# Queries of five heads as seven block products, the softmax ratio on GpSimd, and a step of attention in a lone unit's gap

## The chip, the cores and the metric

The kernel runs on one core of a Trainium2 chip. Its time is the device time of one execution in microseconds (us). Five engines matter: TensorE (PE in the profile, PEld for its weight loads), VectorE (DVE), ScalarE (ACT), GpSimd (POOL) and SyncE (SP), which issues most DMAs. Each engine runs its own list of instructions strictly in the order of that list and waits, where an operand isn't there yet, with all that stands behind it.

## The reference

A trunk of two layers on 16 learned meta tokens and 512 tokens of width 1024: first gated linear attention, then differential attention. The change is in the second layer, cut here to its core:

```python
proj = xn @ w_in                                  # (528, 1024) @ (1024, 8192)
q, k, v, z = jnp.split(proj, 4, axis=-1)          # 8 heads, two maps of 128 each
lam = exp(sum(lv[0]*lv[1])) - exp(sum(lv[2]*lv[3])) + lambda_init
# for each block of 128 queries:
s = einsum('bhpqd,bhpkd->bhpqk', qb, kh) * scale + bias   # p: map 0 and map 1
p = softmax(where(dist >= 0, s, -inf))
a = p[:, :, 0] - lam * p[:, :, 1]
o = einsum('bhqk,bhkv->bhqv', a, vh)
o = head_rms(o) * gnorm * (1.0 - lambda_init)
y = silu(z) * o
h = h + y @ w_out
```

## The kernel before

Every fp32 operand of a matmul is split into a high and a low part (ScalarE copies the high part, VectorE subtracts it for the low part, `split`, L276 and L277), and a product is high by high, high by low and low by high.

The eight heads run one after another. TensorE's order is written out by the program: a queue (`Weaver`) holds the projections of the next head as generators, and the loop over heads places the steps of this head's attention between pieces of them. `W.fill(us)` runs pieces from the queue until their written costs have used up `us`. The order of the other engines is made when the program is built, from priorities and assumed durations; it is a fixed list by the time it runs.

A projection of 256 columns is done in one of two ways. Plain (`project`, L421): for each of two halves of 128 columns 24 matmuls, over all tokens at once (512 columns for queries). Or as a `Unit` of seven block products (`product`, L431): tokens and weights are each cut in two by two blocks, VectorE makes sums of weight blocks (L366), and seven products p1 to p7 of 12 matmuls each, over half of the tokens (256 columns, or 264 with meta tokens), stand for eight. ScalarE copies running sums out of a bank as `u` (L452: after p1, p6 and p7, which add up in one bank bx), and VectorE forms the four outputs from a bank and `u` (L477, L479). The weights come as the parts a11, a12, a22 (used in p1, p2, p4), s21 (p5, p6) and s43 (p7, p3). Only two buffers exist for the last kind, so s43 is made when an earlier pair has been used up. p3 adds up in p5's bank bv, once VectorE has read it for p7's output.

A unit whose successor in the queue is a unit too runs that one's p1 inside itself. A unit that was begun so (`early`) and has no unit behind it is called lone here: its order is p6, p5, p7, p2, p4, p3.

In the second layer gates (z), values (v) and keys (k) are units, in that order, and queries (q) are plain in all heads; from head 2 on each head begins with the output projection of an earlier pair of heads (`q_diff_out2`, its matmuls at L400), and in head 6 the order is k, q, v, z.

Attention of a block of 128 queries has four steps: A (`scores`: for both maps the scores on TensorE at L400, evicted with the bias and the running minimum by VectorE at L1692, the exponential with its sum on ScalarE at L1694; then the ratio of the sums at L1697 and L1698 and the combined tile at L1699), B (`turn`, transposes, L1707), C (`values`, with a power on GpSimd for the norm, L1730), E (`rows`, L1737 and L1740). They are placed as A3 A2 B3 A1 C3 B2 E3 A0 C2 B1 E2 C1 B0 E1 C0 E0, by blocks counted from 0.

The gate unit's p5, as it is written before:

```python
            def p5():
                self.bv = pb_tile("bv")
                yield from product(self.bv, ws.use(s21)[1], X["t1"])
```

## Time and profile before

| what | value |
|---|---|
| time, median of 3 runs (lowest to highest) | 971.22 us (970.94 to 971.46) |
| the profiled execution's own time | 970.65 us |
| its span in the trace | 968.9 us |
| TensorE busy | 957.2 us (99%) |
| VectorE busy | 778.6 us (80%) |
| ScalarE busy | 626.8 us (65%) |
| GpSimd busy | 44.9 us (5%) |
| granted TensorE clock | 0.999 |

The span is the time from the first to the last instruction; what is missing to the execution's time lies around it. Busy times are unions of the instructions' durations on an engine. Matmuls overlap in the array, so for TensorE the distance from start to start tells the cost, not the duration of one.

### The profile page before, as it was taken

Reading aid. Unit: us, or ns where it says so; the run is one execution under the profiler, and the core shown is the slowest. Engines: PE = TensorE matmul, PEld = TensorE weight load, DVE = VectorE, ACT = ScalarE, POOL = GpSimd, SP = SyncE. Lnnn points to the kernel's source line nnn. Section 1 sums busy time; section 2 is a strip of 40 time slices with the busy share of each in tenths; the row PEclk is TensorE's granted clock in tenths of the full one; section 3 lists DMA queues with packets and bytes.
Section 4 is the critical chain, followed back from the end, with each engine's and each line's share of the span. In section 5 each row is a group of like instructions: output and inputs, shape, how many; then the busy total and the mean of one; then the engine's idle time right before and its main releaser. Section 6 shows DMA issues by size and latency. Waiting matters only on the chain.

```text
span 968.9 us, 18048 instructions
## 1 busy us (share of the span) xinstructions
PE 957.2 (99%) x6993; PEld 906.9 (94%) x6993; DVE 778.6 (80%) x1586; ACT 626.8 (65%) x1304; POOL 44.9 (5%) x68
## 2 busy tenths in 40 slices
PE   9999999999999999999999999999999999999997
PEld 8999999999999999998899998998999989989996
DVE  7989885886888787668997987968869769687785
ACT  7776755577647567656757776575675756755583
POOL 1000000000000000000001001000000000000001
PEclk9999999999999999999999999999999999999999
DMA  7322223635363236124355525243342341722212
GB/s 197 88 85 59 82 79 122 147 103 128 116 162 91 85 117 158 53 101 152 99 130 138 143 73 133 75 139 98 99 138 88 118 119 44 182 70 84 89 64 87
DMA packets 128522, 104.94 MB, mean 108 GB/s; under 512 B 51102, under 2 KB 112830, under 8 KB 128433
## 3 DMA queue, kind: packets, MB, share of 16 engines
q1 hardware_dynamic: 123104, 93.80, 35.1%
q10 hardware_dynamic: 5328, 9.95, 2.8%
q8 instruction: 56, 0.92, 0.4%
q14 instruction: 34, 0.27, 0.1%
HBM read 83.64 MB, written 11.80 MB: 99 GB/s over the span
## 4 chain that ended last, share of the span: by engine, by line
PE 88%; ACT 1%; DVE 1%; issue 1%; POOLq 0%; DVEq 0%
PE bx L431 19%; PE bv L431 12%; PE by L431 10%; PE bx L421 10%; PE ps L400 9%; PE bx L972 5%; PE bx L400 3%; PE bv L972 2%; PE by L972 2%; PE ps L1214 2%; PE by L400 2%; PE bv L400 2%; PE ps L1807 1%; PE bx L1807 1%; PE bv L421 1%; PE by L421 1%
## 5 line engine op out<-in xcount | busy, mean ns | idle before, releaser
L277 DVE TENSOR_TENSOR wl<-raw,wh 128x1024 fp32r<-128x1024 f32 x98 | 119.4, 1221 | 23.0 <-ACT wh L276 18.9
L276 ACT ACTIVATE wh<-raw 128x1024 fp32r<-128x1024 f32 x98 | 103.1, 1054 | 48.3 <-PE by L972 22.9
L431 PE MATMUL bv<-x,wh 128*128 128x264 f32 (+1 forms) x656 | 98.6, 287 | 0.0
L431 PE MATMUL bx<-x,wh 128*128 128x264 f32 (+1 forms) x640 | 95.6, 286 | 0.0
L431 PEld LDWEIGHTS bv<-x,wh 128*128 128x128 f32 x656 | 86.8, 189 | 0.6 <-DVE z L479 0.2
L431 PEld LDWEIGHTS bx<-x,wh 128*128 128x128 f32 x640 | 84.6, 188 | 0.7 <-ACT u L452 0.2
L452 ACT ACTIVATE u<-bx 128x264 f32<-128x264 f32 (+1 forms) x120 | 45.3, 379 | 35.5 <-PE bx L431 33.1
L1694 ACT ACTIVATE p<-p,st 128x528 f32<-128x528 f32 (+3 forms) x64 | 36.5, 570 | 41.7 <-DVE st L1692 41.4
L421 PE MATMUL bx<-x,wh 128*128 128x512 f32 (+1 forms) x256 | 62.4, 385 | 0.0
L277 DVE TENSOR_TENSOR wl<-sum,wh 128x1024 fp32r<-128x1024 f32 x41 | 50.1, 1221 | 10.6 <-ACT wh L276 10.5
L431 PE MATMUL bx<-x,wl 128*128 128x264 f32 (+1 forms) x320 | 54.1, 284 | 0.0
L431 PE MATMUL bv<-x,wl 128*128 128x264 f32 (+1 forms) x328 | 53.8, 284 | 0.1
L421 PEld LDWEIGHTS bx<-x,wh 128*128 128x128 f32 x256 | 44.4, 188 | 7.8
L276 ACT ACTIVATE wh<-sum 128x1024 fp32r<-128x1024 f32 x41 | 43.1, 1051 | 9.7 <-PE by L972 3.9
L431 PE MATMUL by<-x,a12h 128*128 128x264 f32 (+1 forms) x320 | 47.5, 286 | 0.1
L1730 POOL TENSOR_TENSOR st<-st,mhalf 128x1 f32<-128x1 f32 x32 | 25.5, 795 | 468.6 <-ACT on L1728 418.2
L431 PE MATMUL bx<-x,a11h 128*128 128x264 f32 (+1 forms) x320 | 46.6, 284 | 0.0
L431 PEld LDWEIGHTS bv<-x,wl 128*128 128x128 f32 x328 | 45.4, 188 | 0.3 <-issue 0.3
L431 PEld LDWEIGHTS bx<-x,wl 128*128 128x128 f32 x320 | 45.3, 188 | 0.3
L431 PEld LDWEIGHTS bx<-x,a11h 128*128 128x128 f32 x320 | 42.4, 188 | 0.6
L431 PEld LDWEIGHTS by<-x,a12h 128*128 128x128 f32 x320 | 42.1, 188 | 0.3 <-ACT t L1658 0.3
L276 ACT ACTIVATE a11h<-raw 128x512 fp32r<-128x512 f32 x41 | 25.7, 626 | 20.7 <-DMA raw<-in_diff_w_in_dram 7.9
(493 smaller groups left out, 2631.9 us busy)
## 6 DMA issues: line engine op xcount, KB each, us to landing
raw<-in_gla_w_in_dram SPq DMA_DIRECT2D x48, 512.0 KB, 4.5
raw<-in_diff_w_in_dram SPq DMA_DIRECT2D x42, 512.0 KB, 4.9
raw<-in_diff_w_in_dram SPq DMA_DIRECT2D x11, 1024.0 KB, 5.9
raw<-in_gla_w_out_dram SPq DMA_DIRECT2D x8, 1024.0 KB, 5.8
raw<-in_diff_w_out_dram SPq DMA_DIRECT2D x8, 1024.0 KB, 6.0
vd<-planes ACTq DMA_DIRECT2D x12, 268.0 KB, 5.8
vd<-keep ACTq DMA_DIRECT2D x12, 264.0 KB, 2.3
T<-bdr SPq DMA_DIRECT2D x8, 264.0 KB, 4.7
```

The costliest lines, as they stand in the source:

```text
L276: act.activation(hi, src, AF.Copy)
L277: dve.tensor_tensor(lo, src, hi.bitcast(F32), op=ALU.subtract)
L400: pe.matmul(ps, l, r, start=first and n == 0, stop=last and n == 2, **kw)
L421: pe.matmul(bank, a[:, k, :], b[k] if n0 is None else b[k][:, n0 + i * nn:n0 + (i + 1) * nn], start=n == 0 and ks[0] == 0, stop=n == len(t ...
L431: pe.matmul(bank[:, :x[q].shape[2]], w[p][:, k * P:(k + 1) * P], x[q][:, k, :], start=first and i == 0, stop=i == len(PASSES) - 1, skip_gr ...
L452: W.moved = act.activation(t, self.bx[:, :self.n], AF.Copy, scale=self.sc)
L972: pe.matmul(banks[i][:, :HT], h.t[p][:, k, mm * P:(mm + 1) * P], s.y[q][k][:, i * HT:(i + 1) * HT], start=n == 0, stop=n == len(PASSES) - 1)
L1214: pe.matmul(o, s.kd[:, i, kc], s.qs[:, i, t0:t0 + n], start=i == 0, stop=i == 1)
L1694: act.activation(p[:, :nk], p[:, :nk], AF.Exp, scale=-1.0, bias=st[:, m:m + 1], accum_out=st[:, 2 + m:3 + m])
L1730: pool.tensor_tensor(ms, ms, mhalf[:, :1], op=ALU.pow)
L1807: pe.matmul(ps[i], yp[hd][p][:, k, b * P:(b + 1) * P], wt[q][cs.start // 512][:, 2 * hd + k, cs.start % 512:(cs.stop - 1) % 512 + 1], star ...
```

## The change

The queries of heads 3 to 7 become units on the 256-column halves of the tokens: their outputs are formed in two ordinary tiles, which are then split into high and low parts (`tail`, one half after p4, the other after p3). Heads 0 to 2 keep the plain product. The unit is entered into the queue with a cost of 8.9 for 10.3.

The scores of map 1 are computed before those of map 0. The ratio of the two sums is made on GpSimd by three instructions of one column (a power with exponent -1, two products) in place of two on VectorE.

A lone unit's p5 marks its last piece as a `Gap`, and `fill` ends there if less than 1.6 is left to fill, or goes on to that place if it is less than 1.6 away; so the attention step that is due stands between p5 and p7. The first fill of each head is 4.0 for 3.0.

```diff
             us -= c
             self.left -= c
             self.spent(c)
+            if isinstance(c, Gap) and us < 1.6:
+                return
+            if us <= 0 and 0 < getattr(self.queue[0], "to_gap", 0) < 1.6:
+                us = 0.01
...
+class Gap(float):
+    pass
...
             def p5():
                 self.bv = pb_tile("bv")
-                yield from product(self.bv, ws.use(s21)[1], X["t1"])
+                alone = early and nxt is None
+                self.to_gap = 1.4 if alone else 0
+                for c in product(self.bv, ws.use(s21)[1], X["t1"]):
+                    self.to_gap -= c
+                    if alone and self.to_gap < 0.2:
+                        self.to_gap = 0
+                        c = Gap(c)
+                    yield c
...
     def q_diff_q(hd, s):
+        scale, qts = -float(P) ** -0.5, []
+        def tiles():
+            assert not hd or heads[hd - 1].scored
+            s.q = [T(ep, [P, 2, NR], F32R, f"q{j}", bufs=1) for j in range(2)]
+        if hd in (3, 4, 5, 6, 7):
+            def dst():
+                tiles()
+                qts.extend([tok_tile()[:, :NR], tok_tile()[:, :NR]])
+                return qts
+            @soon
+            def tail(i):
+                split(*[t[:, i, :] for t in s.q], qts[i])
+            return W.add(Unit(want_unit(d_w_in, 256 * hd), Xr, scale, dst, tail), 8.9)
         want_diff(256 * hd)
...
-            for m in range(2):
+            for m in (1, 0):
...
-            dve.reciprocal(st[:, 5:6], st[:, 3:4])
-            dve.scalar_tensor_tensor(st[:, 5:6], st[:, 5:6], lam, st[:, 2:3], op0=ALU.mult, op1=ALU.mult)
+            pool.tensor_tensor(st[:, 5:6], st[:, 3:4], minus, op=ALU.pow)
+            pool.tensor_tensor(st[:, 4:5], st[:, 2:3], lam, op=ALU.mult)
+            pool.tensor_tensor(st[:, 5:6], st[:, 5:6], st[:, 4:5], op=ALU.mult)
             dve.scalar_tensor_tensor(r.p[0], r.p[1], st[:, 5:6], r.p[0], op0=ALU.mult, op1=ALU.subtract)
...
-        W.fill(3.0)
+        W.fill(4.0)
```

The order of the instructions, before and after, at three places of head 4. After the change all lines have moved: L400 is L409, L421 is L430, L431 is L440, L276 and L277 are L285 and L286, L366 is L375, L452 is L461, L477 is L486, L1692 is L1726, L1694 is L1728, L1699 is L1734, L1723 is L1758 and L1737 is L1772; the ratio stands at L1731 to L1733.

TensorE at the queries of head 4, with a step C of head 3 among them. Before, it stands between the plain matmuls:

```order
L421 MATMUL bx_11878<-x_1514_8556,wh_11770 128x512
L421 MATMUL bx_11878<-x_1515_8557,wh_11770 128x512
L400 MATMUL ps_11898<-v_2004_11223,aT_2124_11853 128x256
L400 MATMUL ps_11898<-v_2005_11224,aT_2124_11853 128x256
L400 MATMUL ps_11898<-v_2004_11223,aT_2125_11854 128x256
L1723 MATMUL ps_11898<-vm_11225,am_11852 128x256
L421 MATMUL bx_11878<-x_1514_8556,wh_11770 128x512
L421 MATMUL bx_11878<-x_1515_8557,wh_11770 128x512
L421 MATMUL bx_11878<-x_1514_8556,wh_11770 128x512
L421 MATMUL bx_11878<-x_1515_8557,wh_11770 128x512
L421 MATMUL bx_11878<-x_1512_8554,wl_11771 128x512 x4
```

After, the step stands ahead of p6 of the query unit (wh and wl on bx), a step E between its p5 (on bv) and p7:

```order
L409 MATMUL ps_11990<-v_2018_11305,aT_2143_11938 128x256
L409 MATMUL ps_11990<-v_2019_11306,aT_2143_11938 128x256
L409 MATMUL ps_11990<-v_2018_11305,aT_2144_11939 128x256
L1758 MATMUL ps_11990<-vm_11307,am_11937 128x256
L440 MATMUL bx_11926<-x_1542_8787,wh_11903 128x256 x8
L440 MATMUL bx_11926<-x_1542_8787,wl_11904 128x256 x4
L440 MATMUL bv_12028<-x_1541_8786,wh_11903 128x256 x8
L440 MATMUL bv_12028<-x_1541_8786,wl_11904 128x256 x4
L1772 MATMUL ps_12041<-ident,on_11995 128x128 x2
L440 MATMUL bx_11926<-x_1543_8788,wh_12001 128x256 x8
L440 MATMUL bx_11926<-x_1543_8788,wl_12002 128x256 x4
L440 MATMUL by_12067<-x_1514_8558,a12h_11907 128x256
```

The plain matmuls on 512 columns are gone, and the steps C and E that stood among them now stand around the unit's p6 and p5.

ScalarE at the gate unit of head 4, where block 1's exponentials (128x272) stand. Before:

```order
L276 ACTIVATE a12h_12223<-raw_11979 128x512 [waits DMAHW2_49,PE_49]
L452 ACTIVATE u_12204<-bx_12120 128x256 [waits PE_49]
L1694 ACTIVATE p_12184,st_12183<-p_12184,st_12183 128x272 [waits DVE_49,Activation_49]
L1694 ACTIVATE p_12191,st_12183<-p_12191,st_12183 128x272 [waits DVE_49]
L276 ACTIVATE wh_12219<-sum_12152 128x1024 [waits PE_49]
L452 ACTIVATE u_12239<-bx_12120 128x256 [waits PE_49]
```

After:

```order
L285 ACTIVATE a12h_12380<-raw_12133 128x512 [waits DMAHW4_49,PE_49]
L1728 ACTIVATE p_12337,st_12336<-p_12337,st_12336 128x272 [waits DVE_49,Activation_49]
L461 ACTIVATE u_12361<-bx_12276 128x256 [waits PE_49]
L1728 ACTIVATE p_12344,st_12336<-p_12344,st_12336 128x272 [waits DVE_49]
L285 ACTIVATE wh_12376<-sum_12308 128x1024 [waits PE_49]
L461 ACTIVATE u_12415<-bx_12276 128x256 [waits PE_49]
```

The copy `u` of the bank that p6 left (the first of the two u rows) stood ahead of both exponentials; now it stands between them.

VectorE where block 0's scores (128x144) are evicted, with the addition of the value unit's p7 from bank bv. Before:

```order
L277 TENSOR_TENSOR a12l_12418<-raw_12117,a12h_12417 128x512
L1692 ISA p_12395,st_12387<-ps_12396,T_11624 128x144 [waits PE_49]
L1692 ISA st_12387 128x1
L277 TENSOR_TENSOR wl_12414<-sum_12335,wh_12413 128x1024 [waits PE_49,Activation_49]
L1697 RECIPROCAL st_12387<-st_12387 128x1 [waits Activation_49]
L477 SCALAR_TENSOR_TENSOR t_12378<-bv_12380,u_12433 128x264 [waits Activation_49]
L1698 SCALAR_TENSOR_TENSOR st_12387<-st_12387,lam 128x1 [waits DVE_49]
L1699 SCALAR_TENSOR_TENSOR p_12388<-p_12395,st_12387,p_12388 128x144 [waits DVE_49]
```

After:

```order
L286 TENSOR_TENSOR a12l_12577<-raw_12273,a12h_12576 128x512
L1726 ISA p_12543,st_12535<-ps_12544,T_11708 128x144 [waits PE_49]
L1726 ISA st_12535 128x1
L1734 SCALAR_TENSOR_TENSOR p_12543<-p_12536,st_12535,p_12543 128x144 [waits Activation_49,Pool_49]
L286 TENSOR_TENSOR wl_12573<-sum_12493,wh_12572 128x1024 [waits PE_49,Activation_49]
L486 SCALAR_TENSOR_TENSOR t_12557<-bv_12559,u_12592 128x264 [waits Activation_49]
```

The combined tile (L1734), which waits for GpSimd, and the part wl of the key unit's s21 now stand ahead of that addition, which before came between the two ratio instructions.

More of the change, by code (lines that the diff above doesn't have):

```diff
@@ L625, in trunk @@
     dve.memset(mhalf, -0.5)
+    minus = cp.tile([P, 1], F32, name="minus")
+    dve.memset(minus, -1.0)
     warm = ps_tile()
@@ L1668, in gen @@
                 yield from project(ws.take(), real2, None, NR, [by_halves(bank)])
-                assert not hd or heads[hd - 1].scored
                 if i == 0:
-                    s.q = [T(ep, [P, 2, NR], F32R, f"q{j}", bufs=1) for j in range(2)]
-                urgent(split)(*[t[:, i, :] for t in s.q], bank, scale=-float(P) ** -0.5)
+                    tiles()
+                urgent(split)(*[t[:, i, :] for t in s.q], bank, scale=scale)
         return W.add(gen(), 10.3)
@@ L1683, in scores @@
             r.st = st = T(ep, [P, 8], F32, "st", bufs=4)
-            r.p = []
+            r.p = [None, None]
             ko = L - nk
-            for m in range(2):
+            for m in (1, 0):
                 p = T(ep, [P, L], F32, "p", bufs=3)
@@ L1694, in scores @@
                 act.activation(p[:, :nk], p[:, :nk], AF.Exp, scale=-1.0, bias=st[:, m:m + 1], accum_out=st[:, 2 + m:3 + m])
-                r.p.append(p[:, :nk])
-            dve.reciprocal(st[:, 5:6], st[:, 3:4])
-            dve.scalar_tensor_tensor(st[:, 5:6], st[:, 5:6], lam, st[:, 2:3], op0=ALU.mult, op1=ALU.mult)
+                r.p[m] = p[:, :nk]
+            pool.tensor_tensor(st[:, 5:6], st[:, 3:4], minus, op=ALU.pow)
+            pool.tensor_tensor(st[:, 4:5], st[:, 2:3], lam, op=ALU.mult)
+            pool.tensor_tensor(st[:, 5:6], st[:, 5:6], st[:, 4:5], op=ALU.mult)
             dve.scalar_tensor_tensor(r.p[0], r.p[1], st[:, 5:6], r.p[0], op0=ALU.mult, op1=ALU.subtract)
```

## The prediction

> **What bounds the kernel now.** I read the page first (busy times, the chain of waits), then the windows of one head's period, then the order of time around one head's queries and around the places where TensorE comes close to waiting. Line numbers in quoted rows are those of the kernel before. The page:
>
> ```profile
> PE 957.2 (99%) x6993; PEld 906.9 (94%) x6993; DVE 778.6 (80%) x1586; ACT 626.8 (65%) x1304; POOL 44.9 (5%) x68
> PE 88%; ACT 1%; DVE 1%; issue 1%; POOLq 0%; DVEq 0%
> ```
>
> TensorE is busy 99% of the span and carries 88% of the chain that ended last, so the kernel ends when TensorE's stream of matmuls ends. Time is won by a shorter stream and lost by a hole in it. The period of head 4, from its queries' first matmul to the next head's (columns: window, then busy time of PE, PEld, DVE, ACT, POOL):
>
> ```profile
> 714.59:777.66 63.07, 63.07 (x436) 58.69 (x435) 50.21 (x109) 41.06 (x93) 3.15 (x4) 1.00 0.36 107
> ```
>
> No hole there at a granted clock of 1.00; VectorE is busy 80%, ScalarE 65%.
>
> **What TensorE saves.** Queries by the plain product, then the first block products of a gate unit on the same 256-column tokens (start, duration; starts are what counts, since durations overlap):
>
> ```profile
> 542.96 3.88 PE L421 MATMUL bx<-x,wh 128*128 128x512 f32 x16
> 546.67 1.32 PE L421 MATMUL bx<-x,wl 128*128 128x512 f32 x5
> 548.75 1.11 PE L431 MATMUL bx<-x,a11h 128*128 128x256 f32 x8
> 550.17 1.11 PE L431 MATMUL by<-x,a12h 128*128 128x256 f32 x8
> ```
>
> Sixteen 512-column matmuls take 3.71 us from start to start, 0.232 each; a head's plain queries are 48 of them, 11.13 us. Twelve 256-column matmuls take 1.42 us, 0.118 each; seven block products are 84, 9.94 us. That is 1.19 us per head and 5.97 us for five heads, all on the engine that sets the end.
>
> **What the others are given.**
>
> ```profile
> L277 DVE TENSOR_TENSOR wl<-raw,wh 128x1024 fp32r<-128x1024 f32 x98 | 119.4, 1221 | 23.0 <-ACT wh L276 18.9 <-PE bx L421 2.9 <-ACT vm L408 0.7
> L277 DVE TENSOR_TENSOR a11l<-raw,a11h 128x512 fp32r<-128x512 f32 x41 | 28.1, 686 | 12.4 <-ACT a11h L276 12.2
> L366 DVE TENSOR_TENSOR sum<-raw 128x512 f32<-128x512 f32 x41 | 28.1, 686 | 7.0 <-DMA raw<-in_gla_w_in_dram 4.1 <-DMA raw<-in_diff_w_in_dram 2.6
> L479 DVE TENSOR_TENSOR t<-bv,u 128x264 f32<-128x264 f32 x26 | 11.1, 428 | 2.9 <-PE bv L431 2.9
> L276 ACT ACTIVATE a11h<-raw 128x512 fp32r<-128x512 f32 x41 | 25.7, 626 | 20.7 <-DMA raw<-in_diff_w_in_dram 7.9 <-PE bx L431 6.5 <-DMA raw<-in_gla_w_in_dram 5.1
> L452 ACT ACTIVATE u<-bx 128x264 f32<-128x264 f32 x99 | 37.3, 379 | 22.5 <-PE bx L431 20.0 <-DVE t L1094 1.1 <-DVE ks L836 0.9
> ```
>
> On VectorE a head's plain queries have two 1024-wide low parts, 2.44 us. The unit has two of these, three of 512 and four 512-wide sums (7 x 0.686 = 4.80), and four additions of the outputs (1.71); the split of the queries themselves costs the same in both. So +6.5 us per head. Taken away are two small ratio instructions per block:
>
> ```profile
> 748.33 0.15 DVE L1697 RECIPROCAL st<-st 128x1 f32<-128x1 f32 x1
> 748.77 0.50 DVE L1699 SCALAR_TENSOR_TENSOR p<-p,st,p 128x272 f32<-128x272 f32 x1
> ```
>
> From the reciprocal to the combination that uses the ratio passes 0.44 us, times four blocks 1.8 us per head. VectorE then has 50.2 + 6.5 - 1.8 = 54.9 us in a period of 61.9: 89%. ScalarE gets three 512-wide copies and three partial copies, 3.0 us: 71%. Both still fit, so neither becomes the bound by its sum; what counts is what stands late at one place. The two weight DMAs of 512 KB replace one of 1 MB on the same SP queue: the same bytes in the same place of the queue, no cost. The wider first fill (4.0 for 3.0) asks for pieces of 1.4 us: three of them either way in heads that begin with an output projection, so nothing there; in heads 0 and 1 a microsecond of products that are due anyway goes ahead of the first scores. The gap edit lets the attention's last step stand between two products of a lone unit. In the rows before no lone unit leaves a hole, so I give it nothing; if the running bank's copy is late there, it covers 0.2 us of TensorE.
>
> **Where a hole opens: the second product of the gate unit.** The scores of block 1 are placed into the gate unit's sixth product. Around it in head 4 (bank bx is then copied by ScalarE as u, before the seventh product may go on in it):
>
> ```profile
> 744.79 0.91 PE L400 MATMUL ps<-k,q 128*128 128x272 f32 x6
> 745.89 1.10 PE L431 MATMUL bv<-x,wh 128*128 128x256 f32 x8
> 747.31 1.10 PE L431 MATMUL bx<-x,wh 128*128 128x256 f32 x8
> ...
> 746.40 0.43 DVE L1692 CUSTOM_DVE_ANT_0 p<-ps,T 128x272 f32<-128x272 f32 x1
> ...
> 746.09 0.39 ACT L452 ACTIVATE u<-bx 128x256 f32<-128x256 f32 x1 [2.00 <-PE bx L431]
> 746.94 0.52 ACT L1694 ACTIVATE p<-p,st 128x272 f32<-128x272 f32 x1 [0.46 <-DVE st L1692]
> 747.46 0.51 ACT L1694 ACTIVATE p<-p,st 128x272 f32<-128x272 f32 x1
> ```
>
> Before, u stands ahead of both exponentials and is done at 746.48, 0.83 us before the seventh product starts. In the changed order of ScalarE one exponential of this block stands ahead of u, in heads 2, 3, 4 and 5. So u, and with it TensorE, waits for the eviction of the scores by VectorE, which is a busy engine there: eviction to exponential 0.54, exponential to the next instruction 0.52, copy 0.39, together 1.45 us. The same two events in heads 2, 3 and 5 (eviction, seventh product):
>
> ```profile
> 620.16 0.43 DVE L1692 CUSTOM_DVE_ANT_0 p<-ps,T 128x272 f32<-128x272 f32 x1
> 621.35 1.10 PE L431 MATMUL bx<-x,wh 128*128 128x256 f32 x8
> 683.00 0.43 DVE L1692 CUSTOM_DVE_ANT_0 p<-ps,T 128x272 f32<-128x272 f32 x1
> 684.22 0.98 PE L431 MATMUL bx<-x,wh 128*128 128x256 f32 x7
> 810.95 0.43 DVE L1692 CUSTOM_DVE_ANT_0 p<-ps,T 128x272 f32<-128x272 f32 x1
> 810.45 1.10 PE L431 MATMUL bx<-x,wh 128*128 128x256 f32 x8
> ```
>
> If VectorE evicts as late as before, the holes are 620.16 + 1.45 - 621.35 = 0.26, then 0.23, 0.54 and 1.95 us: 3.0 in all. How late VectorE will be I can't read. By counting its rows from the end of the queries to this eviction at the spacings of these rows, I get a shift between -0.9 (less ratio work ahead of it) and +1.1 us (the gate's weights come later, since the unit gives its weight buffer back later). The bounds of the term are thus 0.5 (only head 5 keeps a hole) and 7.4 us; I take the middle case of no shift, since work of both signs is added ahead of it.
>
> **The ratio on GpSimd.** The nearest rows are its powers of one column, a copy, and what happens when VectorE is busy beside them:
>
> ```profile
> L1730 POOL TENSOR_TENSOR st<-st,mhalf x32: 548/563/2269, 518.8 to 954.4; 128x1 f32<-128x1 f32 x32
> 13.94 0.24 POOL L774 COPY y<-t 128x64 f32<-128x64 f32 x1 [1.30 <-PE by L717]
> 570.63 2.27 POOL L1730 TENSOR_TENSOR st<-st,mhalf 128x1 f32<-128x1 f32 x1 [24.76 <-ACT on L1728]
> 570.67 1.22 DVE L277 TENSOR_TENSOR wl<-sum,wh 128x1024 fp32r<-128x1024 f32 x1
> 571.81 0.68 DVE L366 TENSOR_TENSOR raw<-raw,sum 128x512 f32<-128x512 f32 x1
> 751.66 0.19 ACT L1728 ACTIVATION_READ_ACCUMULATOR on<-ps 128x1 f32 x1
> 751.99 1.08 POOL L1730 TENSOR_TENSOR st<-st,mhalf 128x1 f32<-128x1 f32 x1 [32.36 <-ACT on L1728]
> ```
>
> The inverse (a power, 0.55) runs beside the other map's exponential; two products remain behind the last exponential. ScalarE's end to GpSimd's start is 0.14 us. A product has no row: between the copy's 0.24 and the power's 0.55, so 0.7 to 1.35 us for hops and two products, against 0.44 before. I take 1.0, the middle: half a microsecond more. The combined tile is needed by transposes some 5 us later, so TensorE doesn't wait for it directly; behind it on VectorE stand weight parts and one addition that frees bank bv for the value unit's third product:
>
> ```profile
> 763.41 0.41 DVE L477 SCALAR_TENSOR_TENSOR t<-bv,u 128x264 f32<-128x264 f32 x1
> 765.82 1.14 PE L431 MATMUL bv<-x,wh 128*128 128x264 f32 x8
> ```
>
> It has 2.0 us to spare before; now combination (0.37) and a low part (1.2) stand ahead of it too, and it waits for the chain above: I come to 764.8 to 765.5, just in time. For this and the query tail (its last split is due when the scores of map 0 start, with well under 1 us to spare by the same count) I add 0.5 us (bounds 0 and 4, a microsecond a head).
>
> While VectorE runs instructions with two SBUF inputs, a power took 2.27 us in place of 0.55 and ended 0.4 us after them. By the Trainium skill, "SBUF — State Buffer", Who interferes with whom, such a VectorE instruction and a GpSimd instruction reading SBUF exclude each other for a whole instruction; the trace agrees for GpSimd, and by this rule the change is worse than I sum it, as in the slower rival below. By the Trainium skill, "GPSIMD Engine Reference", Elementwise side-by-side cycle accounting, an addition of 2048 elements takes 4497 ns at about 2.6 cycles each, which leaves some 60 ns for the fixed part (an estimate): the products would then be nearly free and the sum 0.5 us lower; no row here shows it.
>
> **The sum.** 970.65 us is the profiled execution's time: -5.97 + 3.0 + 0.5 = -2.5, so 968.2. The median of the runs shown is 0.57 above the profiled one: 968.7.
>
> **The rivals.** (1) All is hidden: VectorE's lighter ratio lets it evict 0.5 us sooner or more in every head, and only head 5 keeps a hole: 0.5 us lost, 971.2 - 5.5 = 965.7, down to 965.2 with none. For it: VectorE has 20% idle; against it: it stood at its limit just there. (2) The holes eat all: evictions 0.7 us later in four heads and 0.6 us a head at bank bv, 3.0 + 2.8 + 2.4 = 8.2 lost against 6.0: 973.4; in the middle of this case 971.5, no change. (3) Slower: GpSimd is starved by VectorE's two-input instructions as at 570.63, 1.72 us more in one chain ahead of the eviction of heads 2 to 5, VectorE standing idle behind it: 3.0 + 0.5 + 6.9 = 10.4 lost, 971.2 + 4.4 = 975.6. It decides from 0.65 us a head on. Against it: where VectorE itself waits for the ratio, it does not starve GpSimd. (4) That the queries don't get shorter is excluded by the two rows of starts, unless the unit's matmuls are spaced wider.
>
> **How the numbers follow.** What this measurement can tell from no change is about 0.2%, 1.9 us: faster is below 969.3, slower above 973.2. The forecast, 967 to 970.5 by itself, has 0.48, of which 0.33 is faster; all hidden 0.23, faster; holes eat all 0.16, of which 0.02 is slower; starved 0.13, slower. That is 0.56, 0.29, 0.15. The range from 964.9 (all hidden) to 972.8 leaves out 0.15 above and a little below.
>
> **What the profile after would show.** Query groups of 128x256 at 0.118 us in heads 3 to 7; TensorE idle before the gate's seventh product "until ACT u", largest in head 5; VectorE waiting for POOL st at the combination for about 0.5 to 1 us, four times a head; periods of heads 3 to 5 near 62.5 us for 63.1. The forecast is wrong if the wait for u isn't there (then 965 to 966), or if VectorE's wait at the combination is over 1.5 us in the busy stretch.

## The result and the profile after

The changed kernel takes 975.32 us (median of 6 runs, 974.13 to 976.69) beside 971.08 us for the kernel before on the same chip: ratio 1.0045, 95% interval 1.0033 to 1.0056. It is slower by 4.4 us, where 968.7 was forecast. The profiled execution took 975.16 us with a span of 973.4 us, 4.5 us over the one before, at a granted clock of 0.998 against 0.999.

From the page of the changed kernel, the engines' busy times and the chain that ended last:

```profile
PE 954.2 (98%) x7173; PEld 912.6 (94%) x7173; DVE 798.3 (82%) x1578; ACT 640.0 (66%) x1334; POOL 83.2 (9%) x164
PE 65%; DVE 11%; ACT 7%; DMA 4%; issue 2%; POOL 1%; POOLq 0%; SPq 0%; DVEq 0%; ACTq 0%
```

TensorE has less to do (957.2 before) and yet ends later. Its share of the chain fell from 88% to 65%; VectorE has 11% for 1%, ScalarE 7% for 1%. These are shares of a chain of links and not of waiting time: TensorE is idle 19.2 us of its span for 11.7 before. DMA, which showed no share, has 4%: loads of 3.9 to 6.6 us, most of them of weights, are now links of the chain; one starts at 787.02 us, when a low part of VectorE ends. The prediction gave these loads no cost; no run tests them by themselves.

Where it waits is read from windows that begin at each head's first scores (columns as in the prediction: width, then busy time of PE, PEld, DVE, ACT, POOL; the width less PE's busy time is a hole). Before, the first layer with all that stands ahead of head 0's scores, and then heads 2 to 7:

```profile
0.00:500.14 500.14, 495.47 (x3829) 478.60 (x3830) 409.45 (x763) 326.37 (x599) 16.69 (x32) 1.00 0.39 110
...
604.97:667.87 62.90, 62.90 (x436) 58.67 (x434) 50.51 (x110) 41.15 (x92) 2.87 (x4) 1.00 0.36 109
667.87:730.90 63.03, 63.03 (x436) 58.70 (x434) 49.96 (x109) 41.14 (x92) 2.97 (x4) 1.00 0.35 107
730.90:793.99 63.09, 63.09 (x435) 58.70 (x434) 48.76 (x108) 40.86 (x92) 3.15 (x4) 1.00 0.37 107
793.99:857.03 63.04, 63.04 (x435) 58.74 (x434) 48.92 (x107) 39.20 (x90) 2.61 (x4) 1.00 0.41 113
857.03:911.82 54.79, 54.57 (x330) 48.19 (x329) 43.88 (x95) 29.99 (x74) 2.44 (x4) 1.00 0.26 81
911.82:961.84 50.02, 50.02 (x341) 46.00 (x339) 37.62 (x92) 31.41 (x83) 4.27 (x7) 1.00 0.22 79
```

The same windows of the changed kernel:

```profile
0.00:504.13 504.13, 496.62 (x3838) 479.36 (x3839) 411.00 (x767) 326.88 (x600) 16.73 (x32) 1.00 0.39 109
...
608.40:670.59 62.19, 62.15 (x471) 59.84 (x470) 50.37 (x104) 41.29 (x94) 7.50 (x16) 1.00 0.35 104
670.59:734.78 64.19, 62.78 (x472) 59.91 (x470) 56.45 (x116) 43.35 (x98) 8.77 (x16) 1.00 0.36 106
734.78:797.83 63.05, 62.35 (x471) 59.94 (x470) 55.02 (x114) 43.59 (x99) 7.64 (x16) 1.00 0.37 108
797.83:860.33 62.50, 62.16 (x472) 59.93 (x471) 52.82 (x109) 42.72 (x98) 7.79 (x16) 1.00 0.39 111
860.33:917.91 57.58, 56.10 (x388) 51.82 (x387) 49.51 (x102) 35.50 (x84) 7.23 (x16) 1.00 0.25 78
917.91:966.05 48.14, 47.72 (x319) 43.47 (x318) 35.97 (x84) 29.77 (x82) 9.44 (x19) 1.00 0.24 84
```

The 4.5 us divide so. Ahead of head 0's scores 3.99 are lost, a place where the prediction looked for nothing; 1.4 of them stand already at TensorE's 101st matmul (18.10 us against 16.69). That is start-up which the change does not touch: it is 18.12 in the profile of the ratio alone and 16.57 to 17.07 in the other fifteen. From there to head 0's scores the kernel before takes 483.45 us and the changed one 486.03. The kernels below without the wider fill and without the gap edit in the first layer take 483.1 to 484.1, those with one of the two 484.0 to 484.8, and the four with both 485.1 to 486.4. So these 2.6 us are mostly the fill's and the gap edit's: about 1.1 are nine matmuls that the wider fill put ahead of these scores (3838 for 3829), the rest is holes. Heads 0 and 1 (windows not shown, 104.27 for 104.83) give 0.56 back. Heads 2 to 5 take 251.93 for 252.06: of the 4.8 us that four query units take off TensorE's work, 0.13 is left. Heads 6 and 7 take 0.91 more, and the end from the last matmul's start on 0.29.

What VectorE waits for at the ratio, in total, times and longest (of the changed kernel, then of the kernel before):

```profile
DVE p L1734 <- POOL st L1733: 19.2, 28, 2.5
```

```profile
DVE st L1697 <- ACT p L1694: 9.4, 11, 1.8
```

That is 0.69 us at each of 28 combinations, inside the half to one microsecond that the prediction named. The error was to think that it would cost next to nothing. The start of head 3 shows why (changed kernel, in order of time):

```profile
677.07 1.22 DVE L286 TENSOR_TENSOR wl<-sum,wh 128x1024 fp32r<-128x1024 f32 x1
677.18 1.15 POOL L1732 TENSOR_TENSOR st<-st,lam 128x1 f32<-128x1 f32 x1 [1.12 <-ACT p L1728]
...
678.42 0.19 POOL L1733 TENSOR_TENSOR st<-st 128x1 f32<-128x1 f32 x1
...
678.64 0.77 DVE L1734 SCALAR_TENSOR_TENSOR p<-p,st,p 128x528 f32<-128x528 f32 x1 [0.35 <-POOL st L1733]
...
679.33 0.57 DVE L1726 CUSTOM_DVE_ANT_0 p<-ps,T 128x400 f32<-128x400 f32 x1
...
680.32 0.68 DVE L1818 TENSOR_TENSOR keep<-keep,bx 128x512 f32<-128x512 f32 x1
...
681.05 0.62 PE L440 MATMUL bx<-x,a11h 128*128 128x256 f32 x3 [0.90 <-DVE keep L1818]
```

VectorE waits 0.35 us for GpSimd with two evictions and the sums of the output projection (`keep`) queued behind; the first of these sums frees bank bx, and the gate unit's first product stands 0.90 us waiting for it. Of the kernels below only those with both the units and the ratio on GpSimd have this hole. The wait of 0.35 us is a part of it only.

At the place of which the prediction spoke, the seventh product of the gate unit, head 4 shows what was foreseen: eviction, exponential, copy `u`, product.

```profile
750.65 0.43 DVE L1726 CUSTOM_DVE_ANT_0 p<-ps,T 128x272 f32<-128x272 f32 x1
...
751.18 0.52 ACT L1728 ACTIVATE p<-p,st 128x272 f32<-128x272 f32 x1 [3.17 <-DVE st L1726]
...
751.70 0.36 ACT L461 ACTIVATE u<-bx 128x256 f32<-128x256 f32 x1
...
752.12 1.22 PE L440 MATMUL bx<-x,wh 128*128 128x256 f32 x8 [0.70 <-ACT u L461]
```

Eviction to product takes 1.47 us (1.45 was worked out). From here on a hole is the excess of the distance from start to start over the usual one; it is some 0.16 us more than the idle time in brackets, since a matmul's record outlasts the spacing. Here the holes are 0.21, 0.57, 0.86 and 0.51 us in heads 2 to 5, together 2.15 for the 3.0 forecast; the largest is in head 4 and not, as forecast, in head 5 (1.95).

### The profile page after: what moved, and what is told of

Its sections match the earlier page's. It is cut to its first block, busy times and chain, and to the rows that moved or that the text cites. A ratio compares the mean times of both kernels' runs of the same rounds, so it can differ in the third digit from the quotient of the medians.

```text
span 973.4 us, 18533 instructions
## 1 busy us (share of the span) xinstructions
PE 954.2 (98%) x7173; PEld 912.6 (94%) x7173; DVE 798.3 (82%) x1578; ACT 640.0 (66%) x1334; POOL 83.2 (9%) x164
## 4 chain that ended last, share of the span: by engine, by line
PE 65%; DVE 11%; ACT 7%; DMA 4%; issue 2%; POOL 1%; POOLq 0%; SPq 0%; DVEq 0%; ACTq 0%
PE bx L440 17%; PE by L440 10%; PE bv L440 10%; PE ps L409 7%; PE bx L430 4%; PE bx L990 3%; DMA raw<-in_diff_w_in_dram 2%; DVE wl L286 2%; PE by L990 2%; PE bv L990 2%; PE ps L1232 2%; ACT wh L285 1%; DVE sum L375 1%; ACT p L1728 1%; DMA raw<-in_gla_w_in_dram 1%
## 5 line engine op out<-in xcount | busy, mean ns | idle before, releaser
L285 ACT ACTIVATE wh<-raw 128x1024 fp32r<-128x1024 f32 x93 | 97.9, 1054 | 46.2 <-PE by L990 19.7
L286 DVE TENSOR_TENSOR wl<-raw,wh 128x1024 fp32r<-128x1024 f32 x93 | 113.4, 1221 | 15.8 <-ACT wh L285 14.5
L440 PE MATMUL bv<-x,wh 128*128 128x264 f32 (+1 forms) x736 | 109.3, 286 | 0.0
L440 PE MATMUL bx<-x,wh 128*128 128x264 f32 (+1 forms) x720 | 106.9, 286 | 1.5 <-ACT u L461 1.5
L440 PEld LDWEIGHTS bv<-x,wh 128*128 128x128 f32 x736 | 96.7, 188 | 0.7 <-DVE z L488 0.3
L440 PEld LDWEIGHTS bx<-x,wh 128*128 128x128 f32 x720 | 94.6, 188 | 2.8 <-ACT u L461 2.3
L461 ACT ACTIVATE u<-bx 128x264 f32<-128x264 f32 (+1 forms) x135 | 51.2, 380 | 28.9 <-PE bx L440 27.2
L286 DVE TENSOR_TENSOR wl<-sum,wh 128x1024 fp32r<-128x1024 f32 x46 | 56.2, 1221 | 12.0 <-ACT wh L285 11.9
L1728 ACT ACTIVATE p<-p,st 128x528 f32<-128x528 f32 (+3 forms) x64 | 36.4, 569 | 40.9 <-DVE st L1726 40.7
L440 PE MATMUL bv<-x,wl 128*128 128x264 f32 (+1 forms) x368 | 61.2, 285 | 0.1
L440 PE MATMUL bx<-x,wl 128*128 128x264 f32 (+1 forms) x360 | 59.1, 284 | 0.0
L440 PE MATMUL bx<-x,a11h 128*128 128x264 f32 (+1 forms) x360 | 54.0, 286 | 0.9 <-DVE keep L1818 0.9
L285 ACT ACTIVATE wh<-sum 128x1024 fp32r<-128x1024 f32 x46 | 48.4, 1053 | 9.8 <-PE bv L440 6.9
L440 PE MATMUL by<-x,a12h 128*128 128x264 f32 (+1 forms) x360 | 53.4, 286 | 0.6 <-DVE tick L632 0.5
L440 PEld LDWEIGHTS bv<-x,wl 128*128 128x128 f32 x368 | 51.1, 188 | 0.4 <-issue 0.3
L440 PEld LDWEIGHTS bx<-x,wl 128*128 128x128 f32 x360 | 50.0, 188 | 0.3
L440 PEld LDWEIGHTS bx<-x,a11h 128*128 128x128 f32 x360 | 48.0, 188 | 1.9 <-DVE keep L1818 1.3
L440 PEld LDWEIGHTS by<-x,a12h 128*128 128x128 f32 x360 | 47.1, 189 | 1.1 <-DVE tick L632 0.7
L285 ACT ACTIVATE a11h<-raw 128x512 fp32r<-128x512 f32 x46 | 28.9, 629 | 27.5 <-DMA raw<-in_gla_w_in_dram 9.9
L1731 POOL TENSOR_TENSOR st<-st,minus 128x1 f32<-128x1 f32 x32 | 20.8, 651 | 287.0 <-ACT p L1728 234.8
L558 POOL TENSOR_TENSOR st<-st,mhalf 128x1 f32<-128x1 f32 (+1 forms) x20 | 12.1, 606 | 388.0 <-DVE st L557 388.0
L286 DVE TENSOR_TENSOR a11l<-raw,a11h 128x512 fp32r<-128x512 f32 x46 | 31.6, 687 | 10.9 <-ACT a11h L285 10.3
```

The lines of the kernel that those rows point to most:

```text
L285: act.activation(hi, src, AF.Copy)
L286: dve.tensor_tensor(lo, src, hi.bitcast(F32), op=ALU.subtract)
L440: pe.matmul(bank[:, :x[q].shape[2]], w[p][:, k * P:(k + 1) * P], x[q][:, k, :], start=first and i == 0, stop=i == len(PASSES) - 1, skip_gr ...
L461: W.moved = act.activation(t, self.bx[:, :self.n], AF.Copy, scale=self.sc)
L558: pool.tensor_tensor(dst, dst, mhalf[:np_, :dst.shape[1]], op=ALU.pow)
L1728: act.activation(p[:, :nk], p[:, :nk], AF.Exp, scale=-1.0, bias=st[:, m:m + 1], accum_out=st[:, 2 + m:3 + m])
```

## The experiments

Each was timed beside the kernel before on the same chip. Microseconds against the kernel before are the ratio's distance from 1 times 971; an interval is 0.9 to 1.5 us to each side, so a difference of two kernels is uncertain by 1.2 us or more.

| kernel | ratio (95% interval) | us against before |
|---|---|---|
| the whole change | 1.0045 (1.0033 to 1.0056) | +4.4 |
| units alone | 1.0003 (0.9994 to 1.0012) | +0.3 |
| ratio on GpSimd alone | 1.0073 (1.0059 to 1.0087) | +7.1 |
| gap edit alone | 1.0011 (1.0001 to 1.0020) | +1.1 |
| map order and fill 4.0 | 1.0015 (1.0006 to 1.0024) | +1.5 |
| fill 4.0 alone | 1.0006 (0.9997 to 1.0015) | +0.6 |
| units of heads 3 to 6 | 1.0008 (0.9999 to 1.0016) | +0.8 |
| units and map order | 0.9980 (0.9971 to 0.9988) | -1.9 |
| these and fill 4.0 | 1.0001 (0.9988 to 1.0014) | +0.1 |
| these and the gap edit | 1.0019 (1.0010 to 1.0028) | +1.8 |
| these and the gap edit, second layer only | 1.0010 (1.0001 to 1.0019) | +1.0 |
| these and the ratio on GpSimd | 1.0036 (1.0025 to 1.0047) | +3.5 |
| ratio on GpSimd, map order, fill 4.0 | 1.0055 (1.0041 to 1.0068) | +5.3 |
| the change, ratio back on VectorE | 1.0024 (1.0015 to 1.0034) | +2.3 |
| the change without the gap edit | 1.0028 (1.0018 to 1.0038) | +2.7 |
| the change, map 0 first again | 1.0097 (1.0081 to 1.0112) | +9.4 |
| the change, one product behind the last exponential | 1.0028 (1.0018 to 1.0037) | +2.7 |

**The parts alone.** Units only:

```diff
+        if hd in (3, 4, 5, 6, 7):
+            ...
+            return W.add(Unit(want_unit(d_w_in, 256 * hd), Xr, scale, dst, tail), 8.9)
```

> The kernel before with one part of the change: queries of heads 3 to 7 as units. Theory 1 (each part has a price of its own, and the saving is real): TensorE's stream is 6 us shorter, the ratio stays on VectorE and its waits don't arise; 965.5 to 968.5 us. Rival theory 2 (the units make VectorE and the weight buffers late, and eat their own saving): 970 to 974 us, with holes on TensorE after the query units in heads 3 to 6.

Measured 970.71 us, +0.3: the second theory. 6.0 us of work are gone and the time stands still. In its profile 460.49 us pass from head 0's first scores to the last matmul, for 461.69 before, so 4.8 us of the 6.0 are waited away; holes of 0.12 us and more are 3.8 of them. One of the places:

```profile
666.04 1.22 DVE L277 TENSOR_TENSOR wl<-raw,wh 128x1024 fp32r<-128x1024 f32 x1
...
667.17 0.68 DVE L277 TENSOR_TENSOR q<-t,q 128x512 fp32r<-128x512 f32 x1
...
667.91 1.48 PE L400 MATMUL ps<-k,q 128*128 128x264 f32 x10 [0.42 <-DVE q L277]
```

The last low part of the queries stands behind a weight part, and the first scores wait for it; head 4 has the same (a hole of 0.56 us, 0.57 here). The others are 0.92 us at a product of head 3's gate unit, which waits for ScalarE's copy `u`, 0.92 and 0.76 us in head 6 and 0.44 us in head 7. The plain product splits straight out of the bank, while the unit puts an addition into a tile in between.

Ratio only:

```diff
-            dve.reciprocal(st[:, 5:6], st[:, 3:4])
-            dve.scalar_tensor_tensor(st[:, 5:6], st[:, 5:6], lam, st[:, 2:3], op0=ALU.mult, op1=ALU.mult)
+            pool.tensor_tensor(st[:, 5:6], st[:, 3:4], minus, op=ALU.pow)
+            pool.tensor_tensor(st[:, 4:5], st[:, 2:3], lam, op=ALU.mult)
+            pool.tensor_tensor(st[:, 5:6], st[:, 5:6], st[:, 4:5], op=ALU.mult)
```

> The kernel before with only the ratio of sums on GpSimd. Theory 1: VectorE waits for GpSimd at the combined tile four times a head, some of it shows on TensorE as holes: 972 to 974 us. Rival theory 2: hidden, 970.5 to 971.5 us.

Measured 978.78 us, +7.1, the dearest part by far. TensorE's order is that of before, so the whole difference is waiting. Its list of waits (total, times, longest):

```profile
PE bx L431 <- ACT u L452: 6.3, 5, 1.7
```

With the excess over the usual spacing these five holes are 7.1 us. Here map 0 comes first, so the power stands behind the last exponential, and VectorE waits 33.1 us in 32 combinations. Behind it the evictions are late, behind them ScalarE, and there the copy `u`.

Gap edit only (the two pieces of the diff above that name `Gap` and `to_gap`):

> The kernel before with only the gap edit (a step placed between p5 and p7 of a lone unit), first fill still 3.0. The order of TensorE changes already in the first layer, since its lone units have the mark too. Theory 1: the 1.5 us that the changed kernel is behind at the end of the first layer, start-up left out, come from this: 972 to 973.5 us. Rival theory 3 (that difference is jitter of the start-up loads and of one execution): 970.5 to 971.5 us.

Measured 971.79 us, +1.1. The prediction had missed that the first layer has lone units too. Its trace has two holes that the kernel before has not, both there, and none in the second layer; the larger:

```profile
109.91 0.68 ACT L1271 ACTIVATE t<-ps,st 16x512 f32<-16x512 f32 x1 [0.20 <-POOL st L558]
...
110.64 0.42 PE L1324 MATMUL ps<-ident,t 16*128 16x16 f32 x4 [0.52 <-ACT t L1271]
```

The edit moves the step of the first layer's attention that is due in a lone unit's p5 to that product's end, and the steps that follow (L1230 there, L1214 before) stand six matmuls later each. The transposes above stand where they stood, but ScalarE comes to their operand at 109.91 us for 108.96 (L1271 there, L1255 before), and TensorE waits for it.

Map order and fill:

```diff
-            for m in range(2):
+            for m in (1, 0):
-        W.fill(3.0)
+        W.fill(4.0)
```

> The kernel before with only map 1's scores ahead of map 0's and the first fill of 4.0. Theory 1: if ScalarE's order again has one exponential of block 1 ahead of the copy of the gate unit's bank, holes of about 0.2 to 0.9 us in heads 2 to 5, 972 to 974 us. Rival theory 2: the order alone costs nothing, 970.5 to 971.5 us.

Measured 972.49 us, +1.5. Then the fill by itself:

> The kernel before with the first fill of each head at 4.0 for 3.0 and nothing else. Theory 1 (the 1.4 us that map order and fill cost together are the fill's, which in heads 0 and 1 puts products ahead of the first scores): 972 to 972.6. Theory 2 (they are the map order's, which changes which exponential stands in front): 970.7 to 971.3.

Measured 971.96 us, +0.6 with an interval that holds zero. The map order with plain queries thus costs 0.9 us by this difference, not to be told from nothing. The four single prices add to 10.0 us; together they cost 4.4.

**One part taken back from the change.** Ratio on VectorE again (the ratio diff above, reversed):

> The changed kernel with the ratio back on VectorE; units, gap, map order and fill kept. Theory 1 (the ratio's way over GpSimd is the dear part: VectorE waits 19.2 us for it in the changed kernel against 9.4 for the exponential before, and the 2.15 us of TensorE's holes ahead of the gate unit's seventh product are its work): 970.5 to 972.5. Theory 2 (the units' lateness and the other two edits cost the time, the ratio is hidden): 974 to 976.

Measured 973.63 us: 2.1 us better than the change, and still 2.3 over before, between the two theories. The gap edit out:

> The changed kernel without the gap edit. Theory 1 (the gap edit only disturbs the first layer's order, as it does alone, and does nothing useful in the second): about 1 us less than the changed kernel, 974 to 974.8. Theory 2 (in the second layer it covers waits that the units bring): no gain or a loss, 975.2 to 977.

Measured 974.13 us, 1.7 us better: the first theory. The profiles agree: without the edit the stretch ahead of head 0's scores, start-up left out, is 1.2 us shorter, and the one behind it is not (462.58 us to the last matmul, 461.92 in the change). Map 0 first again (`for m in range(2)`):

> The changed kernel with the first map's scores first again; fill 4.0 kept. Theory 1 (the map order takes the inverse, 0.55 us on GpSimd, out of the chain behind the last exponential; without it VectorE waits 0.5 us more in each of 32 blocks, as where the ratio is moved alone, and TensorE's holes at the seventh product return): 978 to 981. Theory 2 (the map order costs what it costs alone, 1 to 1.7 us, whatever stands beside it): 973.5 to 974.5.

Measured 980.57 us, 5.0 us worse than the change: the first theory. VectorE's wait at the combination rises again:

```profile
DVE p L1734 <- POOL st L1733: 26.5, 28, 2.7
```

So map order, next to nothing by itself, is worth 5 us in the change. It takes the power out of the chain behind the last exponential: with map 0 first the holes at the gate's seventh product are 4.21 us for 2.15. And it has the queries ready in time: with map 0 first the first scores of heads 3 and 4 wait for a low part again (0.60 and 0.46 us), as with the units alone. The reverse, ratio with map order and fill but plain queries (`if hd in ()`):

> Ratio on GpSimd, second map first and fill 4.0, queries all by the plain product, no gap edit. Theory 1 (with the inverse out of the chain the ratio on GpSimd costs little beyond the map order's own 1.7 us): 972.5 to 974.5, holes ahead of the seventh product of 2 us in all. Theory 2 (any way over GpSimd holds VectorE at the combination, the plain queries give no time back): 977 to 980.

Measured 976.39 us, +5.3, between the two ranges: 3.8 over map order and fill alone, less than the 7.1 of the ratio with map 0 first, but not little.

**The length of GpSimd's chain.** The inverse is multiplied by lambda while the other exponential runs, so that one product remains behind it:

```diff
-            pool.tensor_tensor(st[:, 4:5], st[:, 2:3], lam, op=ALU.mult)
-            pool.tensor_tensor(st[:, 5:6], st[:, 5:6], st[:, 4:5], op=ALU.mult)
+            pool.tensor_tensor(st[:, 5:6], st[:, 5:6], lam, op=ALU.mult)
+            pool.tensor_tensor(st[:, 5:6], st[:, 5:6], st[:, 2:3], op=ALU.mult)
```

> The changed kernel, GpSimd's two products in another order: the inverse times lambda first, beside the first map's exponential, so that one product and not two stands behind the last exponential (0.35 us and a step less in each of 32 chains). Theory 1 (the length of that chain is what the ratio costs, VectorE waits for it 19.2 us in the changed kernel): VectorE's wait falls to 8 to 12 us, time 973.8 to 974.6. Theory 2 (GpSimd is held up by VectorE's instructions, whatever its own number): no change, 975 to 976.

Measured 973.74 us, 1.7 us better than the change, close to the first theory's time. VectorE's wait fell less than it said:

```profile
DVE p L1734 <- POOL st L1733: 17.4, 25, 2.6
```

That a shorter chain helps is not shown by this. Up to head 0's scores, where no ratio is made, TensorE, ScalarE and GpSimd have the same order in both kernels, yet the profile is 2.19 us shorter there (501.94 for 504.13); from there to the last matmul, where the edit acts, it takes 462.17 us for 461.92. What it does show is that nine tenths of the wait remain with one product less, so the number of products is the smaller part of it.

**What the units need.** Units with map order, the ratio on VectorE, no gap edit, fill 3.0:

> Units and map order; ratio on VectorE, no gap edit, fill 3.0. Theory 1 (the units' own two holes of 0.57 and 0.56 us are the scores of the first map waiting for the last low part of the queries; the second map's queries are ready one product earlier, so with map 1 first those holes are gone): 969.3 to 970.3. Theory 2 (the map order costs its own 1 us beside the units too): 971.5 to 972.5.

Measured 969.27 us (12 runs), ratio 0.9980: the first theory, and the only kernel here faster than the one before (by 0.2%). The second map's queries are ready one product earlier, and no scores wait for a low part any more. Its windows, heads 2 to 7:

```profile
605.44:668.34 62.90, 62.12 (x471) 59.75 (x470) 51.41 (x112) 41.31 (x94) 3.34 (x4) 1.00 0.35 103
668.34:731.65 63.31, 62.40 (x472) 59.92 (x470) 56.71 (x124) 43.49 (x98) 3.10 (x4) 1.00 0.36 107
731.65:793.63 61.98, 61.98 (x472) 59.88 (x470) 55.85 (x122) 43.58 (x99) 3.05 (x4) 1.00 0.38 110
793.63:855.49 61.86, 61.86 (x472) 59.85 (x471) 53.37 (x117) 42.77 (x98) 2.67 (x4) 1.00 0.38 112
855.49:911.50 56.01, 54.73 (x378) 50.76 (x377) 48.91 (x107) 34.44 (x83) 2.24 (x4) 1.00 0.24 78
911.50:960.08 48.58, 48.58 (x328) 44.57 (x327) 38.10 (x94) 31.21 (x82) 4.78 (x7) 1.00 0.24 86
```

Heads 4 and 5 run at 61.98 and 61.86 without a hole: the saving of 1.19 a head (61.9 was worked out) is real where nothing waits. Heads 2, 3 and 6 give it away. In head 3 two products of the gate unit wait for ScalarE's copy `u` (holes of 0.50 and 0.73 us, the second at the seventh). At the end of head 2 a wait stands that the prediction had not seen at all:

```profile
666.38 0.42 DVE L481 SCALAR_TENSOR_TENSOR t<-bv,u 128x256 f32<-128x256 f32 x1
...
666.85 0.50 PE L400 MATMUL bv<-wh,hT 128*128 128x512 f32 x1 [0.78 <-DVE t L481]
```

The unit's last output lies in bank bv until VectorE has added it, and the output projection that follows at once wants that bank. In head 6 (the rows are the changed kernel's) sums of weight blocks for head 7's query unit (L375) stand on VectorE ahead of the multiplication by the gate (`yt`) that frees a bank for the next scores:

```profile
884.49 0.68 DVE L375 TENSOR_TENSOR raw<-raw 128x512 f32<-128x512 f32 x1
...
885.10 0.68 DVE L1818 TENSOR_TENSOR keep<-keep,bx 128x512 f32<-128x512 f32 x1
...
885.69 0.41 DVE L1775 TENSOR_TENSOR yt<-ps,z 128x256 f32<-128x256 f32 x1
...
886.16 0.56 PE L409 MATMUL ps<-k,q 128*128 128x144 f32 x3 [0.84 <-DVE yt L1775]
```

Before, VectorE had no such sums there, and the wait was 0.22 us. Units of heads 3 to 6 only (`if hd in (3, 4, 5, 6)`, without map order) were to show whether the loss sits in heads 6 and 7:

> Queries as units in heads 3 to 6 only, nothing else changed. Theory 1 (in heads 3 to 6 the units win 1.5 us by the start of head 6's scores, and the loss is in the end of head 6 and in head 7, where order and cover are others): 969 to 969.8. Theory 2 (a lighter TensorE meets the other engines' own pace: what is won in one head is waited away in the next): 970.4 to 971.

Measured 971.88 us, +0.8, above both ranges; the first theory is wrong. The wait for `yt` is back at 0.23 us, as it should be without sums for head 7, but head 6's window still takes 56.57 us for 54.79: its steps C now wait for low parts of VectorE's (starts 0.88, 0.52 and 0.53 us late). A hole that is closed in one place came up in the next, as the second theory said, though its price was too low.

**What the other parts cost beside the units.** Three single additions to the kernel of 969.27. The ratio on GpSimd:

> Units, map order and the ratio on GpSimd in the change's three instructions; no gap edit, fill 3.0. The ratio's price with the rest quiet. Theory 1 (VectorE's wait for GpSimd opens the holes ahead of the gate unit's seventh product again, 2 to 3 us in four heads): 971 to 972.5. Theory 2 (with the units the combination has time to spare, the ratio is hidden and the loss in the changed kernel is fill and gap): 969 to 970.

Measured 974.22 us, +3.5: 5.4 us for the ratio, more than the first theory had. VectorE waits 20.8 us (30 times) for GpSimd in place of 6.4 (9 times) for the exponential, and the windows of all heads together take 4.8 us more, of 5.2 us between the two spans. Holes in these windows are 7.4 us for 4.0: new are one at the gate's first product in head 3 (1.05), those at the seventh in heads 4 and 5 (0.97 and 0.31), one at head 4's first scores (0.51) and three in head 7 (1.07 together); the two in head 3 of the kernel without come down from 1.23 to 0.55. Fill 4.0:

> Units, map order and fill 4.0; ratio on VectorE, no gap edit. Theory 1 (the fill costs beside the units what it costs alone, 0.6 to 1 us): 969.9 to 970.6. Theory 2 (beside the units' shorter pieces it costs most of the 4.2 us by which ratio on VectorE with gap and fill stands above units with map order): 971.5 to 973.

Measured 970.23 us, ratio 1.0001 with the widest interval of all (0.9988 to 1.0014), 2.0 us over the kernel without by the ratios, with an uncertainty of 1.5; its profiled span was the same (967.3 against 967.4). Beside the ratio on GpSimd the fill goes with a gain of 0.8 (+2.7 for +3.5), less than the uncertainty. Its price is not settled; it is small. The gap edit, in both layers and in the second alone (`alone = early and nxt is None and up[0] is not up1`, whose last condition holds from the second layer on):

> Units, map order and the gap edit in both layers; ratio on VectorE, fill 3.0. Theory 1 (the gap edit costs about 1.1 us as it does alone and as its removal from the changed kernel gives): 970 to 970.8. Theory 2 (most of the 4.2 us is the gap's): 972 to 973.

> As the kernel with units, map order and gap edit, but the gap edit acts in the second layer only. Theory 1 (its price is the changed order of the first layer, holes of 0.25 and 0.69 us there): 968.8 to 969.6, at least 0.7 below the kernel with the gap in both layers. Theory 2 (the price is in the second layer too): as with the gap in both layers, 970 or more.

Measured 972.62 and 972.12 us, +1.8 and +1.0. Both first theories fall: beside the units the gap edit costs 3.7 us and not 1.1, and 2.9 of them are in the second layer. Three holes there are not in the kernel without the edit: 0.38 and 0.62 us in head 4, and the largest, 1.22 us, in head 7. There a step C stands nine matmuls later than without the edit. The following step E keeps its place, and what it needs comes late: VectorE stands waiting for ScalarE at a piece of the gate (L1583) ahead of the multiplication `yt`. From the kernel with the gap in the second layer only:

```profile
937.63 0.69 DVE L1583 SCALAR_TENSOR_TENSOR z<-z,t 128x512 f32<-128x512 f32 x1 [0.91 <-ACT t L1582]
...
938.43 0.42 DVE L1773 TENSOR_TENSOR yt<-ps,z 128x256 f32<-128x256 f32 x1
...
939.00 0.71 PE L409 MATMUL ps<-y,aT 128*128 128x256 f32 x4 [1.06 <-DVE yt L1773]
```

In the whole change its removal gives 1.7, less than 3.7. It may be that one wait covers the other where VectorE is late by the ratio anyway; no run shows that.

## Why the prediction was wrong, point by point

**The step that failed.** The prediction gave the map order, the fill and the gap edit no term, and the ratio together with the query tail 0.5 us; 3.0 of the 3.5 us lost were to sit at one place, the seventh product. One edit after the other, the runs give: units +0.3 us, with map order -1.9, with the ratio on GpSimd +3.5, with the fill +2.7, with the gap edit +4.4 (each step uncertain by 1.2 us or more, and other orders would share the sum out otherwise). So the units with map order win 1.9 us, not far from the 2.5 forecast, but their holes stand elsewhere. The ratio, at 5.4 us in this order, is the term that turns the gain into a loss, and the gap edit, at 1.7, the second.

**What TensorE saves: right.** 1.19 us a head, and heads 4 and 5 of the kernel with units and map order run at 61.98 and 61.86.

**"Both still fit, so neither becomes the bound by its sum": right as a sum, and the step that misled.** VectorE was to have 54.9 us in the period of head 4 and has 55.02 in head 4's window (55.09 from its query unit's p6 to the next one's). But TensorE waits at single places for one late instruction of VectorE or ScalarE, and VectorE is 81 to 88% busy in heads 2 to 6 of the changed kernel. The prediction examined three such places: the seventh product, bank bv before p3, and the query tail. The second and third have no hole in the changed kernel. The units alone lost their saving at the first scores of heads 3 and 4, at another product of the gate, where ScalarE was the late one, and in heads 6 and 7.

**The seventh product: the chain of waits right, the sum near, the spread not.** 2.15 us of holes for 3.0, with 0.51 for 1.95 in head 5, so that the sum came near is partly luck. The exponential ahead of `u` doesn't come of the map order: with map order and fill alone `u` stands ahead of both exponentials, as before, and with the units alone or the ratio alone one or both exponentials stand ahead of it. Nor is that order enough. With units and map order one exponential stands ahead of `u` in heads 2, 4 and 5 and both in head 3, and one hole of 0.73 us, in head 3, is left. With the ratio on GpSimd there are three (0.55, 0.97 and 0.31 in heads 3 to 5). It takes the order and an eviction that VectorE makes late. The prediction left open how late VectorE would be; the ratio, by these two runs, is what makes it late in heads 4 and 5.

**The ratio on GpSimd, "half a microsecond more", priced at nothing but a share of the 0.5 us for bank bv and the query tail: the mis-sized term.** It cost 7.1 us alone, 5.4 beside units and map order, 2.1 in the whole change. The wait itself was foreseen (0.69 us a time); that evictions, copies and freed banks stand behind it on VectorE was written for the slower rival alone. This rival, with 975.6 us and a chance of 0.13, came nearest. That its time fits to 0.3 us is luck: in the profile 4.0 of the 4.5 us stand ahead of head 0's scores, where no ratio is made, and its starvation was to be 1.72 us a chain. Of the prediction's two signs of being wrong neither came: the wait for `u` is there, and VectorE's longest wait at the combination in heads 2 to 6 is 1.44 us, under 1.5. What was wrong lay where no sign was set. The view of the product with lambda, minimum, median and maximum in ns:

```profile
L1732 POOL TENSOR_TENSOR st<-st,lam x32: 186/192/1153, 508.8 to 944.5; 128x1 f32<-128x1 f32 x32
```

Half of these products take no more than 0.19 us, but the mean of the 32 is 0.35; the power's mean is 0.65 at a median of 0.55. What these two last beyond their medians is thus some 0.26 us a chain. By the Trainium skill, "SBUF — State Buffer", Who interferes with whom, an instruction of VectorE with two SBUF inputs and one of GpSimd that reads SBUF shut each other out; the row at 677.18 agrees, lasting 1.15 us until VectorE's low part of 677.07 is over, and that low part keeps its 1.22 us. "Where VectorE itself waits for the ratio, it does not starve GpSimd" missed this case: at that row VectorE still had a low part to do ahead of its wait, and starved GpSimd before it began to wait.

**"In the rows before no lone unit leaves a hole, so I give it nothing": wrong.** An edit to the order can also open holes: it moves steps to later places, and a step behind them finds its operand late. That cost 1.1 us alone, in the first layer, which the prediction had not looked at, and 3.7 beside the units.

**The wider fill at nothing: not refuted.** 0.6 us alone, not to be told from zero.

**The map order was given no term of its own.** It is the part that the others need: 2.2 us better beside the units (1.0003 to 0.9980), 5.0 in the whole change, where the ratio gains by it too.

The range ended at 972.8. Each term's bounds were taken by themselves, and the case in which VectorE's waits make several of them worse at once was left to the 0.15 above it. What stays open is the fill's price, and why the parts cost 4.4 us together and 10.0 singly, beyond what the map order does for units and ratio.

## What to carry to other kernels

An engine with a tenth or more of its time free can still hold up another whose banks and operands hang on single instructions in its queue: count what stands behind each new wait, not only how long it lasts. Work moved to another engine to relieve a busy one can cost more than it frees where the busy one waits for its result; here two short instructions on VectorE were cheaper than three on GpSimd with a wait. Test the parts of such a change in company, since two of them (units and map order) gave 1.9 us together, and apart no gain that could be told from zero.

## What was not expected of the hardware

A product of one column on GpSimd takes 0.19 us (32 of them, median 192 ns) where the power takes 0.55; the prediction had put it between 0.24 and 0.55. By the Trainium skill, "GPSIMD Engine Reference", Elementwise side-by-side cycle accounting, the fixed part would have been some 60 ns (the prediction's estimate); the rows show three times that.
